# Hybrid decoder step on one core: where the bias rows are made, and which attention loads go out before the projection ends

## The chip, the core and the metric

The kernel runs on one core of a Trainium2 chip. The core has five engines with instruction streams of their own: TensorE (PE in the profile; its weight loads are PEld), VectorE (DVE), ScalarE (ACT), GpSimd (POOL) and SyncE (SP). SP computes nothing: it issues nearly all DMA transfers, in program order, so a transfer that has to wait holds those behind it. POOL issues the gathers from the paged cache. The metric is the time in microseconds of one execution on the device; shown is the median of several.

## The reference

One layer of a hybrid decoder trunk, for a prompt of 2048 tokens and for a sample group of 8 x 4 tokens with a paged cache of 8192 positions. Cut to what matters here:

```
h = rms_norm(x, pre_g);  z = h @ w_in            # 1024 -> 5632 columns, split into ca cb cg pu pg q k v sg mq mg
y_c = conv_branch(ca, cb)                        # GLU, causal depthwise conv (31), LayerNorm, swish, pointwise
y_p = pool_branch(pu)                            # causal means over 2/4/8/16, needs state_pool (8 x 15 rows) as history
y_s = stick_breaking(q, k, v, sb_bias)           # 8 heads x 64, strictly causal, z = q.k/8 + b_h
y_m = mem_attend(mq, mem_k, mem_v)               # 4 heads x 128, 256 memory tokens
mix = concat(y_c*silu(cg), y_p*silu(pg), y_s*silu(sg), y_m*silu(mg))
y   = rms_norm(x + rms_norm(mix @ w_out, post_g), final_g)

def sb_block(q, k, v, bias, q_pos, k_pos):       # stick-breaking attention
    z = einsum(q, k) * d**-0.5 + bias
    log_1m = where(k_pos < q_pos, log_sigmoid(-z), 0)
    a = exp(where(k_pos < q_pos, log_sigmoid(z) + reverse_cumsum(log_1m) - log_1m, -inf))
    return einsum(a, v)
```

Everything is float32; products are made from a high and a low part of each operand. Outputs are also the new keys and values and the conv and pool histories.

## The kernel before

The program has three stages. In the **projection**, PE multiplies 1024 prompt tokens at a time (part 0, then part 1) with one 128-column group of the combined weight after the other (`z_groups`, L819). At its start eight groups of the memory tokens are mixed in (`mem_tokens`, L418; their product is `mz`), and parameters and histories are loaded as rows and transposed by PE (`params_and_histories`, L474: tiles `ht` and products `hps`). A weight arrives by DMA as `wr`, ACT makes its high part `whi` and POOL its low part `wlo` (L241, L242); each kind has two buffers. Products leave PSUM through ACT and DVE and go to DRAM scratch: `qd` and `kd` (high and low parts of queries and keys), `vd` (values), `gsd` and `gcd` (gates), `ydw` (convolved rows), `mixd` (finished branch outputs). Beside the projection, the sample group's attention over the cache is interleaved step by step (gathers `kt` and `vt` by POOL, transposes `T` by DVE, scores `sSA` and values `sO` by PE).

The second stage is **prompt attention** (`sb_prompt`, L1312). It runs over 16 blocks: four head pairs `hp` times four query blocks `qb` of 512 rows. A block visits its key blocks `kc` from `qb` down to 0, and in each one four row pairs (two heads `hh`, and query tiles 0-1 or 2-3): scores `S` by PE into one of two PSUM banks, two sigmoids by ACT (`gam`, which has three buffers, and `be`; these are called the gates), scans `E` by DVE, a product by POOL, transposes `AT` by PE, a copy `at` by ACT, and the product `av` with the values. `sb_loader` (L1256) loads what a block needs: `load(hp, qb)` issues for each of two heads eight transfers (keys high `kh`, keys low `kl`, queries `Q`, and rows of `bd` that add the bias inside the product), and `values(hp)` one transfer of 1 MB (tile `V`). `bd` is a small DRAM tensor of bias rows, made once by `bias_rows` (L454): a load `brow`, a memset of `brows` on POOL, four small DVE copies and a store on SP. The third stage is the **output projection**.

Between the first two stages stands `sb_early` (L1298). When the sample's attention is done, its memory is closed and a pool `sbr` is opened in its place, while the projection is still running. `sb_early` loads block (0, 0) there and computes the first two row pairs' scores `Se` and gates `early` between the last matmuls of the projection. The pool `sb`, for all else, is opened when the projection's memory is closed, and its tiles take over addresses of projection tiles: who first writes such a tile waits until the old one's last reader is done.

The order on PE is the order of the code. On the other engines a scheduler orders the instructions. Work that is added as a task (`tasks.add`) is stepped in between the projection's steps. Each SP transfer reports on one of eight counters in turn, and waits until the eighth transfer before it has landed.

Of the kernel before, what the change touches and what calls it, by code (L numbers as in the profile page):

```python
# [9 lines left out]
F32R = mybir.dt.float32r  # L10
# [8 lines left out]
P = 128  # L19
# [43 lines left out]
KT = 2  # L63
# [29 lines left out]
def kernel(  # L93
# [9 lines left out]
    pe, act, dve, pool, sp = nc.tensor, nc.scalar, nc.vector, nc.gpsimd, nc.sync  # L103
# [155 lines left out]
    tasks = Tasks()  # L259
# [7 lines left out]
    def k4(name, shape, dt):  # L267
        return st.tile(shape, dt, tag="k4", name=name, bufs=K4)
# [7 lines left out]
    def later_stats():  # L276

        ahead = []
        for t in range(9):
            if t < 8:  # L280
                ahead.append(k4(f"xs1_{t}", [P, D], F32))
                sp.dma_start(ahead[-1], xp[PART + P * t : PART + P * (t + 1), :])
                yield
                yield
            if t:
                row_stats(ahead.pop(0), P, rs1[:, t - 1 : t])
                yield
        rstd(rs1)
# [165 lines left out]
    def bias_rows():  # L454

        b = zc.tile([NH, 1], F32, name="brow")
        sp.dma_start(b, sb_bias.rearrange("o h -> h o"))
        hl = zc.tile([NH, 2], F32R, name="bhl")
        t = k4("brows", [P, 2, 512], F32)
        pool.memset(t[: NH + 1], 1.0)  # L460
        for _ in range(3):
            yield
        dve.tensor_copy(hl[:, 0:1], b)
        dve.tensor_tensor(out=hl[:, 1:2], in0=b, in1=hl[:, 0:1].bitcast(F32), op=ALU.subtract)
        for x in range(2):
            dve.tensor_copy(t[:NH, x], hl[:, x : x + 1].bitcast(F32).to_broadcast([NH, 512]))
        sp.dma_start(bd, t[: NH + 1])
# [788 lines left out]
    def sb_loader(sbr):  # L1256

        KT, V = {}, {}

        def load(hp, qb):  # L1260
            tok = slice(512 * qb, 512 * qb + 512)
            Q = []
            for hh in range(2):
                pr = slice(64 * hh, 64 * hh + 64)
                kts = [(sbr if qb == 0 else KT["pool"]).tile([P, 512], F32R, tag=f"k{n}{qb}", name=f"k{n}{hp}_{qb}_{hh}",
                                                             bufs=2 if qb else 4) for n in "hl"]
                qt_ = sbr.tile([P, 2, 512], F32R, tag="Q", name=f"Q{hp}_{qb}_{hh}", bufs=4)
                for x in range(2):
                    hx = slice(64 * x, 64 * x + 64)
                    sp.dma_start(kts[0][hx].bitcast(F32), kd[hp, pr, 0, tok])  # L1270
                    sp.dma_start(qt_[hx, 0].bitcast(F32), qd[hp, pr, x, tok])
                sp.dma_start(kts[1][:64].bitcast(F32), kd[hp, pr, 1, tok])
                sp.dma_start(qt_[:64, 1].bitcast(F32), qd[hp, pr, 0, tok])
                sp.dma_start(kts[1][64:66].bitcast(F32), bd[2 * hp + hh])
                sp.dma_start(qt_[64:66, 1].bitcast(F32), bd[NH])
                KT[hp, hh, qb] = kts
                Q.append(qt_)
            if qb == 0 and hp:
                values(hp)
            return Q, KT, V  # L1280

        def values(hp):
            V[hp] = sbr.tile([P, 16, P], F32, tag="V", name=f"V{hp}", bufs=2)
            sp.dma_start(V[hp], vd[:, P * hp : P * (hp + 1)].rearrange("(t p) c -> p t c", p=P))

        return load, values

    def sb_scores(S, q2, w, Q, kts):
# [6 lines left out]
        act.activation(out=ga, in_=S[:, :, :w], func=AF.Sigmoid, scale=-1.0)  # L1295
        act.activation(out=be, in_=S[:, :, :w], func=AF.Sigmoid)  # L1296

    def sb_early(load, blk, sbr, bps, early):  # L1298

        room = sbr.tile([P, 16, P], F32, tag="V", name="early", bufs=2).rearrange("p (n j b) c -> p n j (b c)", n=4, j=2)  # L1300
        blk[0, 0] = load(0, 0)
        for _ in range(4):
            yield
        for hh in range(2):
            S = bps.tile([P, 512], F32, tag="AT", name=f"Se{hh}", bufs=2).rearrange("p (j k) -> p j k", j=2)
            Q, KT, _ = blk[0, 0]
            sb_scores(S, 0, 2 * P, Q[hh], KT[0, hh, 0])
            early[hh] = room[:, 2 * hh], room[:, 2 * hh + 1]
            sb_gates(S, 2 * P, *early[hh])
            yield  # L1310

    def sb_prompt(load, loaded, sb, bps, ops, zmp, early, values_of, flags, newest):  # L1312
# [14 lines left out]
        blocks = [(hp, qb) for hp in range(4) for qb in range(4)]  # L1327
# [88 lines left out]
                late.pop(0)[1]()  # L1416

        for bi, (hp, qb) in enumerate(blocks):
            if bi + 1 < len(blocks):
                loaded[blocks[bi + 1]] = load(*blocks[bi + 1])  # L1420
            if bi == 0:
                values_of(0)
            Q, KT, V = loaded[hp, qb]
            V = V[hp]
            gt = sb.tile([P, 512], F32, tag="sgt", name=f"sgt{hp}_{qb}", bufs=1)
            sp.dma_start(gt, gsd[hp, :, 512 * qb : 512 * qb + 512])
            carry = {}
            for kc in range(qb, -1, -1):
                base = step
                for q2 in (0, 2):  # L1430
                    for hh in range(2):
                        cost = 1.33 * (2 * q2 + 3) / 4 if kc == qb else 2.66
                        rest = score(hp, qb, kc, hh, q2, Q, KT, carry)
                        if len(pend) == 2:
                            pend.pop(0)()
                        pend.append(rest)
                        yield cost / 2
                        behind(step)
                        step += 1
                        yield cost / 2  # L1440
                for n, q2 in ((0, 0), (2, 2)):
                    late.append((base + n + TURN + SUM, lambda a=(hp, qb, kc, q2, V, gt): values(*a)))
                    for hh in range(2):
                        late.append((base + n + hh + TURN, lambda a=(hp, qb, kc, hh, q2): turn(*a)))
                late.sort(key=lambda x: x[0])
# [429 lines left out]
    with tc.tile_pool(name="mem", bufs=2, side="right") as mp:  # L1875
        M = {}
        xst = x_first(lambda n: mp.tile([P, D], F32, tag="xt", name=n, bufs=XB))
        for _ in range(X0):
            next(xst)
        tasks.add(xst)  # L1880
        params = params_and_histories(mp)
        for n, _ in enumerate(z_groups(0, GROUPS[0][:1])):
            tasks.step()
            if n in (0, 2):
                tasks.step()
            if n == 4:
                next(params)
            if X["done", 0] >= XM and not M:
                M["gen"] = mem_norm(mp, M)
                tasks.add(M["gen"])  # L1890
        for _ in M["gen"]:
            pass

        sp.dma_start(conv_sample[0][:, 0 : CH - TS, :], state_conv[0][:, TS:CH, :])
        sp.dma_start(pool_sample[0][:, 0 : PH - TS, :], state_pool[0][:, TS:PH, :])
        sp.dma_start(bias_bc, sb_bias[0].partition_broadcast(P))
        tasks.add(bias_rows())
        tasks.add(params)
        mem = mem_tokens(mp, M)
        for _ in z_groups(0, GROUPS[0][1:4], mem):  # L1900
            tasks.step()
        for _ in range(3):
            tasks.step()
# [11 lines left out]
    def main():  # L1915
        yield from z_groups(0, GROUPS[0][4:12])
        tasks.add(later_stats())
        yield from z_groups(0, GROUPS[0][12:])
        tasks.add(state_rows(0))
        yield from z_groups(1, GROUPS[1][:7])  # L1920
        tasks.add(sample_mem())
        yield from z_groups(1, GROUPS[1][7:-2])
        tasks.add(state_rows(1))
        yield from z_groups(1, GROUPS[1][-2:])
# [4 lines left out]
    due, blk, early = 0.0, {}, {}  # L1929
    sbr = bx = None  # L1930
    for cost in main():
        tasks.step()
        due += rate * cost
        while sample is not None and due >= 1.0:
            due -= 1.0
            try:
                next(sample)
            except StopIteration:
                sample = None
                sx.close()  # L1940
                bx = ExitStack()
                sbr = bx.enter_context(tc.tile_pool(name="sbr", bufs=1, side="right", reuse_waits="tile"))
                load, values_of = sb_loader(sbr)
                bps = bx.enter_context(tc.tile_pool(name="bps", bufs=1, space=PSUM, side="right", reuse_waits="tile"))
                starts = sb_early(load, blk, sbr, bps, early)
                next(starts)
                tasks.add(starts)
    tasks.drain()
# [185 lines left out]
    for n, x in enumerate(parts):  # L2134
# [15 lines left out]
        for k, p_ in enumerate(out_part(x) if n >= len(lead_) else lead if not n else ()):  # L2150
# [5 lines left out]
            if not n:  # L2156

                k, at_ = p_ % 4, p_ // 4
# [41 lines left out]
```

## Time and profile before

| | |
|---|---|
| median of 3 runs | 2349.55 us (2348.55, 2349.55, 2355.44) |
| the profiled execution | 2350.55 us |
| its span, first to last instruction | 2348.1 us |
| busy share of the span | PE 96%, DVE 70%, POOL 55%, ACT 48% |
| first matmul of prompt attention (`Se`) | 1475.9 us |
| granted PE clock, mean over the span | 0.990 |

Times in the views are microseconds from the start of the span. A row of instructions has start, duration, engine, line, operation, output <- inputs, and in brackets how long the engine was idle before it and what released it. A row of windows has the stretch and its length, then the busy time of PE, PEld, DVE, ACT and POOL (with instructions), the granted PE clock, the busy share of the DMA engines and GB/s. A row of waits has who waited for what, the total, the count and the longest.

### The profile page before, as it was taken

Reading aid. Unit: us, or ns where it says so; the run is one execution under the profiler, and the core shown is the slowest. Engines: PE = TensorE matmul, PEld = TensorE weight load, DVE = VectorE, ACT = ScalarE, POOL = GpSimd, SP = SyncE. Lnnn points to the kernel's source line nnn. Section 1 sums busy time; section 2 is a strip of 40 time slices with the busy share of each in tenths; the row PEclk is TensorE's granted clock in tenths of the full one; section 3 lists DMA queues with packets and bytes.
Section 4 is the critical chain, followed back from the end, with each engine's and each line's share of the span. In section 5 each row is a group of like instructions: output and inputs, shape, how many; then the busy total and the mean of one; then the engine's idle time right before and its main releaser. Section 6 shows DMA issues by size and latency. Waiting matters only on the chain. (4 is left out here: it accounts for less than half of the span.)

```text
span 2348.1 us, 43432 instructions
## 1 busy us (share of the span) xinstructions
PE 2246.9 (96%) x16512; PEld 1812.3 (77%) x16512; DVE 1654.7 (70%) x2247; ACT 1125.3 (48%) x2031; POOL 1296.6 (55%) x1410
## 2 busy tenths in 40 slices
PE   7899999999999999999999999799999899999997
PEld 7898888888888777777777777566666667788775
DVE  5332686969757764478787867787877766686997
ACT  6232343242442322224242234699999985453553
POOL 3454545556474656545555454488988863432333
PEclk9999999999999999999999999899999999999999
DMA  6589977878778999987877884576544206976774
GB/s 216 172 269 308 348 264 260 284 261 274 265 249 308 310 355 337 333 278 274 310 255 243 300 274 139 144 208 192 153 126 137 79 19 224 291 229 191 240 246 150
DMA packets 338188, 558.31 MB, mean 238 GB/s; under 512 B 29163, under 2 KB 213611, under 8 KB 321581
## 3 DMA queue, kind: packets, MB, share of 16 engines
q1 hardware_dynamic: 282604, 286.83, 39.5%
q0 software_dynamic: 55376, 268.72, 32.3%
q8 instruction: 130, 2.13, 0.4%
q14 instruction: 78, 0.63, 0.1%
HBM read 465.35 MB, written 90.72 MB: 237 GB/s over the span
## 5 line engine op out<-in xcount | busy, mean ns | idle before, releaser
L990 DVE STREAM_TRANSPOSE T<-kt 128x1024 f32<-128x1024 f32 x256 | 308.7, 1226 | 185.1 <-PE sSA L1003 175.4
L957 POOL DMA_INDIRECT vt<-in_cache_v_dram,idv x256 | 252.4, 986 | 255.4 <-PE sO L1042 194.4
L642 DVE SCALAR_TENSOR_TENSOR cacc<-U,par,cacc 128x512 f32<-128x512 f32 x480 | 360.0, 750 | 11.0
L1372 POOL TENSOR_TENSOR be<-be,E 128x512 f32<-128x512 f32 (+4 forms) x316 | 301.3, 964 | 28.0 <-DVE E L1363 13.8
L1363 DVE TENSOR_TENSOR_SCAN E<-gam,cr,ZM 128x513 f32<-128x513 f32 x192 | 232.7, 1265 | 29.6 <-ACT gam L1295 26.4
L957 POOL DMA_INDIRECT kt<-in_cache_k_dram,idk x128 | 128.2, 1001 | 201.5 <-DVE T L990 159.0
L2019 PE MATMUL acc<-wohi,mh 128*128 128x512 f32 (+1 forms) x480 | 193.5, 403 | 1.1 <-ACT mh L1743 1.1
L2019 PE MATMUL acc<-wolo,mh 128*128 128x512 f32 (+1 forms) x480 | 189.6, 395 | 0.0
L2019 PE MATMUL acc<-wohi,ml 128*128 128x512 f32 x448 | 178.8, 399 | 7.2 <-DVE ml L1754 7.2
L1391 PE MATMUL AT<-ident,be 128*128 128x128 f32 x1082 | 150.0, 278 | 24.3 <-ACT at L1393 17.9
L1295 ACT ACTIVATE gam<-S 128x1024 f32<-128x1024 f32 (+1 forms) x158 | 162.4, 1028 | 17.7 <-PE S L1292 14.3
L1393 ACT COPY at<-AT 128x512 f32<-128x512 f32 (+1 forms) x288 | 161.3, 647 | 18.7 <-PE AT L1391 18.6
L1391 PEld LDWEIGHTS AT<-ident,be 128*128 128x128 f32 x1082 | 118.7, 141 | 66.6 <-issue 28.8
L1296 ACT ACTIVATE be<-S 128x1024 f32<-128x1024 f32 (+1 forms) x158 | 161.6, 1023 | 0.0
L1291 PE MATMUL S<-kh,Q 128*128 128x512 f32 (+1 forms) x316 | 132.0, 422 | 13.2 <-DMA kh<-kd 13.2
L1003 PE MATMUL sSA<-T,W 128*32 128x128 f32 x4096 | 138.4, 276 | 2.0 <-DVE T L990 1.6
L1360 DVE TENSOR_TENSOR_SCAN E<-gam,ZM 128x384 f32<-128x384 f32 (+1 forms) x124 | 95.5, 814 | 60.3 <-ACT gam L1295 57.4
L1403 PE MATMUL av<-at,V 128*64 128x256 f32 (+1 forms) x1152 | 136.3, 377 | 0.0
L1003 PEld LDWEIGHTS sSA<-T,W 128*32 128x32 f32 x4096 | 104.8, 109 | 36.8 <-issue 29.4
L1754 DVE TENSOR_TENSOR ml<-mr,mh 128x512 fp32r<-128x512 f32 x108 | 92.4, 863 | 44.1 <-ACT mh L1743 43.3
L1042 PE MATMUL sO<-vt,saT 128*32 128x512 f32 x1024 | 122.1, 592 | 0.0
L1403 PEld LDWEIGHTS av<-at,V 128*64 128x64 f32 x1152 | 76.1, 137 | 56.7 <-issue 24.8
(590 smaller groups left out, 6176.6 us busy)
## 6 DMA issues: line engine op xcount, KB each, us to landing
mr<-mixd SPq DMA_DIRECT2D x32, 512.0 KB
Q<-qd SPq DMA_DIRECT2D x96, 128.0 KB
mr<-mixd SPq DMA_DIRECT2D x48, 256.0 KB
xtp<-in_x_prompt_dram SPq DMA_DIRECT2D x16, 512.0 KB
kh<-kd SPq DMA_DIRECT2D x64, 128.0 KB
ws<-in_w_out_dram SPq DMA_DIRECT2D x16, 512.0 KB
wsd<-ws SPq DMA_DIRECT2D x16, 512.0 KB
msd<-mr SPq DMA_DIRECT2D x32, 256.0 KB
```

The source lines that it names most:

```text
L642: dve.scalar_tensor_tensor(out=ps, in0=U[:, a + k : a + k + H], scalar=wd[:, k : k + 1], in1=ps, op0=ALU.mult, op1=ALU.add)
L957: pool.indirect_dma_start(out=dst, out_offset=None, in_=rows, in_offset=bass.IndirectOffsetOnAxis(ap=idx, axis=0))
L990: S["turn"] = dve.transpose(T[:, 2 * hh : 2 * hh + 2].rearrange("p s j t -> p (s j t)"), kt[:, 2 * hh : 2 * hh + 2].rearrange("p s j d -> ...
L1003: pe.matmul(sSs[n][32 * g : 32 * g + 32, P * ml : P * (ml + 1)], lhsT=W[:, jj, :], rhs=T[:, :, jj, :], start=i == 0, stop=i == 3, tile_pos ...
L1295: act.activation(out=ga, in_=S[:, :, :w], func=AF.Sigmoid, scale=-1.0)
L1296: act.activation(out=be, in_=S[:, :, :w], func=AF.Sigmoid)
L1363: dve.tensor_tensor_scan(out=E[:, j][:, ::-1], data0=g_[:, j][:, ::-1], data1=ZM[:, 0:1].to_broadcast([P, 513]), initial=carry[hh, q2][:, ...
L1372: newest.append(pool.tensor_tensor(out=be[:, j, :m], in0=be[:, j, :m], in1=E[:, j, 513 - w : 513 - w + m], op=ALU.mult).ins)
L1391: pe.transpose(ap_[:, n : n + P], A[hp, qb, kc, hh, qt][:, P * r : P * (r + 1)], ident)
L1393: act.copy(at[:, :n], ap_[:, :n])
L1403: pe.matmul(av[64 * hh : 64 * hh + 64, c], lhsT=V[:, 4 * kc + r, 64 * hh : 64 * hh + 64], rhs=ats.pop((hp, qb, kc, hh, q2, r)), start=dg a ...
L2019: pe.matmul(o[:rows], lhsT=m[a][:, k, :rows], rhs=W[prod, 4 * h + k][w], start=not cont and h == k == n == 0, stop=h == 1 and k == 3 and n ...
```

## The change

Three edits. The task `bias_rows` is added later: not at the end of the first group but behind the first value groups. In `sb_early`, blocks (0, 0) and (0, 1) are both loaded, and the values of the first head pair behind them; `sb_prompt` no longer loads these itself. For that the key buffers are shared out anew: query block 0 used to have four buffers of each kind in `sbr` and blocks 1 to 3 two each in `sb`; now `sbr` holds two for block 0 (even head pairs) and two for block 1, and `sb` two for block 0 of odd head pairs (slot 4) and two each for blocks 2 and 3. The amount of memory is the same.

```diff
@@ load(hp, qb) in sb_loader
-                kts = [(sbr if qb == 0 else KT["pool"]).tile([P, 512], F32R, tag=f"k{n}{qb}", name=f"k{n}{hp}_{qb}_{hh}",
-                                                             bufs=2 if qb else 4) for n in "hl"]
+                slot = qb if qb or hp % 2 == 0 else 4
+                kts = [(sbr if slot < 2 else KT["pool"]).tile([P, 512], F32R, tag=f"k{n}{slot}", name=f"k{n}{hp}_{qb}_{hh}",
+                                                              bufs=2) for n in "hl"]
@@ sb_early
-    def sb_early(load, blk, sbr, bps, early):
+    def sb_early(load, values, blk, sbr, bps, early):
         room = sbr.tile([P, 16, P], F32, tag="V", name="early", bufs=2).rearrange("p (n j b) c -> p n j (b c)", n=4, j=2)
-        blk[0, 0] = load(0, 0)
+        for n in range(2):
+            blk[0, n] = load(0, n)
+        values(0)
@@ sb_prompt
-            if bi + 1 < len(blocks):
+            if bi + 1 < len(blocks) and blocks[bi + 1] not in loaded:
                 loaded[blocks[bi + 1]] = load(*blocks[bi + 1])
-            if bi == 0:
-                values_of(0)
@@ behind the first group
         sp.dma_start(bias_bc, sb_bias[0].partition_broadcast(P))
-        tasks.add(bias_rows())
         tasks.add(params)
@@ main()
         yield from z_groups(0, GROUPS[0][4:12])
         tasks.add(later_stats())
+        tasks.add(bias_rows())
         yield from z_groups(0, GROUPS[0][12:])
@@ the call
-                starts = sb_early(load, blk, sbr, bps, early)
+                starts = sb_early(load, values_of, blk, sbr, bps, early)
```

How this moves instructions, at three places. First, SP's queue in the first microseconds of the projection, where the pooling history `ht15_0` is loaded. Before:

```order
L492 DMA ht30_4_658<-in_state_conv_dram 120x512
L233 DMA wr0q3_689<-in_w_in_dram 128x8x128
L435 DMA mkd_67<-mhlk0_693 128x512
L467 DMA bd_69<-brows_638 9x1024
L492 DMA ht15_0_721<-in_state_pool_dram 120x512
L450 DMA out_10_dram<-mnat0_726 128x2x128
```

And now:

```order
L492 DMA ht30_4_653<-in_state_conv_dram 120x512
L233 DMA wr0q3_684<-in_w_in_dram 128x8x128
L435 DMA mkd_67<-mhlk0_688 128x512
L492 DMA ht15_0_711<-in_state_pool_dram 120x512
L450 DMA out_10_dram<-mnat0_716 128x2x128
```

The store of the bias rows to `bd` no longer stands ahead of the history's load. Second, SP's queue behind the first value groups, where the store stands now (`xs` are rows of the prompt's second half for `later_stats`, `wr0cg` and `wr0pg` weights); before, the same rows stood there without `bd`:

```order
L282 DMA xs1_1_2724<-in_x_prompt_dram 128x1024
L233 DMA wr0cg0_2506<-in_w_in_dram 128x8x128
L467 DMA bd_69<-brows_2694 9x1024
L282 DMA xs1_2_2809<-in_x_prompt_dram 128x1024
L282 DMA xs1_3_2904<-in_x_prompt_dram 128x1024
L233 DMA wr0pg0_2674<-in_w_in_dram 128x8x128
```

Third, SP's queue at the end of the projection, behind the loads of block (0, 0). In `kh0_1_0` the numbers are head pair, block and head. Before:

```order
L744 DMA gsd_61<-sg1sg3_0_14738 128x512
L744 DMA gcd_60<-sg1cg3_1_14778 128x512
L564 DMA mixd_63<-mo1_3_512_14791 128x4x128
L1271 DMA Q0_1_0_14885<-qd_57 64x512
L649 DMA ydw_62<-acc1_3_1_14854 128x512
```

```order
L744 DMA gsd_61<-sg1sg3_1_14828 128x512
L1284 DMA V0_14905<-vd_59 128x16x128
L1270 DMA kh0_1_0_14883<-kd_58 64x512 x2
L1272 DMA kl0_1_0_14884<-kd_58 64x512
L1274 DMA kl0_1_0_14884<-bd_69 2x512
```

And now (the sixteen loads of block (0, 1) stand ahead of it, the last four of them shown):

```order
L1273 DMA kl0_1_1_14738<-kd_58 64x512
L1274 DMA Q0_1_1_14739<-qd_57 64x512
L1275 DMA kl0_1_1_14738<-bd_69 2x512
L1276 DMA Q0_1_1_14739<-bd_69 2x512
L1285 DMA V0_14748<-vd_59 128x16x128
L744 DMA gsd_61<-sg1sg3_0_14762 128x512
L744 DMA gcd_60<-sg1cg3_1_14802 128x512
L564 DMA mixd_63<-mo1_3_512_14815 128x4x128
L744 DMA gsd_61<-sg1sg3_1_14852 128x512
L649 DMA ydw_62<-acc1_3_1_14878 128x512
L1272 DMA Q0_2_0_14939<-qd_57 64x512 x2
L1274 DMA Q0_2_0_14939<-qd_57 64x512
```

The keys of block (0, 1) and the values moved ahead of five stores of the projection's last results, and the loads of block (0, 2) come right behind these.

## The prediction

> **What bounds the kernel now.** I read the page's busy shares first, then what TensorE (PE) waited for, then windows of the stages that the change touches, and last the rows in order of time around the two longest waits there.
>
> ```profile
> PE 2246.9 (96%) x16512; PEld 1812.3 (77%) x16512; DVE 1654.7 (70%) x2247; ACT 1125.3 (48%) x2031; POOL 1296.6 (55%) x1410
> PE S L1291 <- DMA kh<-kd: 13.2, 1, 13.2
> PE hps L510 <- DMA ht<-in_state_pool_dram: 6.4, 1, 6.4
> 180.00:300.00 120.00, 120.00 (x1112) 107.42 (x1115) 61.61 (x76) 36.79 (x79) 59.31 (x53) 1.00 0.94 326
> 1500.00:1550.00 50.00, 45.46 (x325) 33.16 (x325) 41.41 (x52) 44.16 (x66) 36.06 (x53) 0.96 0.55 136
> ```
>
> PE is busy for 96% of the span, so the time is PE's work plus PE's waits. In the projection it never pauses (120.00 of 120 us) although the DMA engines are 0.94 busy, so what is won before it is still won behind it. In prompt attention PE (45.46 of 50) and ACT (44.16) limit each other. Each wait row gives a total, a count and the longest: two single waits of PE on a DMA, 13.2 and 6.4 us. The change moves what stands ahead of both.
>
> **Part 1: the bias rows leave the early queue.** Rows are start, duration, engine (SPq is SP's queue of DMA issues).
>
> ```profile
> 64.50 0.58 SPq L435 DMA_DIRECT2D mkd<-mhlk  x1
> 71.59 0.28 SPq L467 DMA_DIRECT2D bd<-brows  x1
> 71.97 0.34 SPq L492 DMA_DIRECT2D ht<-in_state_pool_dram  x1
> 70.82 0.74 DVE L466 COPY brows<-bhl 8x512 f32<-8x512 f32 x2
> 67.10 0.38 PE L251 MATMUL z0q<-xhi,whi0q 128*128 128x288 f32 x1
> 68.65 0.29 PE L251 MATMUL z0q<-xhi,wlo0q 128*128 128x288 f32 x1
> 75.35 1.03 PE L510 MATMUL hps<-ident,ht 120*128 120x120 f32 x4 [6.40 <-DMA ht<-in_state_pool_dram]
> 76.46 0.59 PE L251 MATMUL z0q<-xhi,whi0q 128*128 128x288 f32 x1
> 79.48 0.41 PE L251 MATMUL mz<-mhi,whi0mem 128*128 128x256 f32 x1
> 66.00:68.00 2.00, 2.00 (x19) 2.00 (x19) 0.00 (x0) 1.11 (x2) 0.00 (x0) 1.00 0.95 275
> 68.00:70.00 2.00, 0.94 (x8) 0.71 (x6) 1.32 (x1) 0.61 (x2) 1.99 (x1) 1.00 0.22 80
> 76.00:78.00 2.00, 2.00 (x10) 2.00 (x10) 1.18 (x5) 0.00 (x0) 0.00 (x0) 0.50 0.95 264
> ```
>
> SP issues in order. After mkd (ends 65.08) it stands for 6.5 us at the store of bd, which waits for DVE's copies (70.82 to 71.56); the load of ht, the pooling history, comes behind it, and PE's transposes need it. Without bd, ht can go at 65.1. From its issue to PE's start it took 75.35 − 71.97 = 3.4 us, then on idle DMA engines. At 65.1 the weights and mkd are in front of it: the engines are 0.95 busy to 68 and done near 68.4 (0.22 of the next 2 us). 240 KB at 275 GB/s are 0.9 us, so I take 69.4, against 68.8, when PE has finished its group of twelve. The wait falls from 6.4 to about 0.6. Bounds: 68.5 (no wait left) and 71.5 (the busy engines, then the full 3.4 us).
>
> The slow clock goes with the wait. Behind 6.4 us of idling the granted clock is 0.50 (window 76 to 78): the twelve matmuls from 76.46 to 79.48 take 3.02 us, the twelve from 67.10 some 1.68. With the six transposes (75.35 to 76.46, about half of it too much) that is 1.9 us. Hence mz starts at 69.4 + 4.13 − 1.9 = 71.6 in place of 79.48, 7.9 us earlier, and runs on the full clock: its 24 matmuls, 3.44 us here, take 2.81 later (87.34 to 90.15), 0.6 us more. What is late next is the next weight:
>
> ```profile
> 79.48 1.04 ACT L241 CAST whi0q<-wr0q 128x1024 fp32r<-128x1024 f32 x1 [10.84 <-PE z0q L251]
> 80.60 2.39 POOL L242 TENSOR_TENSOR wlo0q<-wr0q,whi0q 128x1024 fp32r<-128x1024 f32 x1 [10.23 <-ACT whi0q L241]
> 82.92 0.34 PE L251 MATMUL z0q<-xhi,whi0q 128*128 128x384 f32 x1
> 83.27 0.34 PE L251 MATMUL z0q<-xhi,wlo0q 128*128 128x384 f32 x1
> 87.34 0.28 PE L251 MATMUL mz<-mhi,whi0mem 128*128 128x256 f32 x1
> 90.15 0.34 PE L251 MATMUL z0q<-xhi,whi0q 128*128 128x384 f32 x1
> ```
>
> ACT's cast starts when PE leaves the old weight and wlo0q is there 3.5 us later (79.48 to 82.99); PE wants it for the third matmul behind mz, 2.81 + 0.35 us on (82.92 to 83.27), so it waits 0.3 us. Part 1 is **−8.2 us**; with ht at 71.5 and a PE that cools again, −4; with no wait at all, −8.8.
>
> The work itself is not saved but moved to the value groups near 240 us: one memset on POOL (0.94 us in its old place), two small DVE copies (0.74), one store of 36 KB. I cost it at nothing. PE runs without a pause there, DVE idles 4.9 us behind the transposes after which the copies now stand, and SP is held there anyway:
>
> ```profile
> 237.05 8.45 SPq L282 DMA_DIRECT2D xs<-in_x_prompt_dram  x2
> 244.13 1.25 DVE L990 STREAM_TRANSPOSE T<-kt 128x1024 f32<-128x1024 f32 x1 [4.88 <-PE sSA L1003]
> 239.52 0.95 POOL L957 DMA_INDIRECT kt<-in_cache_k_dram,idk  x1 [3.34 <-DVE T L990]
> 254.97 2.37 DVE L990 STREAM_TRANSPOSE T<-kt 128x1024 f32<-128x1024 f32 x2 [7.52 <-PE sSA L1003]
> ```
>
> Behind bd on SP are two loads of xs and then the weight wr0pg. POOL too waits there (3.34 us ahead of the gather in front of which the memset now stands). If the cover were gone, the copies' 0.7 us and the memset's 0.9 would be the price.
>
> **Part 2: keys and queries of the second block, and the first values, go out earlier.**
>
> ```profile
> 1463.14 0.52 SPq L1270 DMA_DIRECT2D kh<-kd  x1
> 1472.00 0.25 SPq L1275 DMA_DIRECT2D Q<-bd  x1
> 1484.70 0.39 SPq L1284 DMA_DIRECT2D V<-vd  x1
> 1485.18 4.15 SPq L1270 DMA_DIRECT2D kh<-kd  x2
> 1493.78 0.24 SPq L1274 DMA_DIRECT2D kl<-bd  x1
> 1481.34 0.40 PE L1292 MATMUL S<-kl,Q 66*128 66x512 f32 x1
> 1494.92 0.55 PE L1291 MATMUL S<-kh,Q 128*128 128x256 f32 x1 [13.18 <-DMA kh<-kd]
> 1484.26 1.02 ACT L1296 ACTIVATE be<-S 128x1024 f32<-128x1024 f32 x1
> 1500.21 1.03 ACT L1295 ACTIVATE gam<-S 128x1024 f32<-128x1024 f32 x1 [0.89 <-ACT at L1393]
> 1487.15 1.00 DVE L1360 TENSOR_TENSOR_SCAN E<-early,ZM 128x128 f32<-128x128 f32 x2 [1.80 <-DMA gsd<-sg1sg]
> 1488.07 3.99 DVE L1360 TENSOR_TENSOR_SCAN E<-gam,ZM 128x384 f32<-128x384 f32 x4
> 1514.20 0.37 PE L1291 MATMUL S<-kh,Q 128*128 128x256 f32 x1
> 1484.00:1494.00 10.00, 0.00 (x0) 0.00 (x0) 5.91 (x8) 3.11 (x4) 6.03 (x10) 0.50 0.89 222
> ```
>
> The sixteen loads of the first block are issued from 1463.14 to 1472.25, 9.1 us. The second block's sixteen now follow at once, to about 1481.4, then V. Its first half is issued by 1477 and its second by 1481.4, and 3.4 us more are 1484.8. PE is done with the first block at 1481.7, but not free: its score bank is released only by ACT's be, which ends at 1485.28. So keys are no longer what it waits for. Behind that the third pair of gate buffers must be released by DVE's scans. The scans wait 1.80 us for a store of a projection tile; in the changed order no scan carries such a wait, so they end at 1490.3 instead of 1492.06. The gates of block (0, 1)'s third row pair, at 1500.21 now, could then start at 1490.4: **at best −9.8 us**, from where ACT runs back to back as it does now.
>
> But V now stands ahead of five stores that were issued around it before: gsd, gcd, mixd, gsd, ydw, 256 KB each. In the changed order ACT's first two copies "at" lie on tiles that mixd and ydw read, and wait for these stores. V's landing: the last kl waits for the eighth transfer before it, which is V, until 1493.78, 9 us behind V's issue; the kh issued right behind V freed PE at 1494.92, 1.1 us later still. So V issued near 1481.6 lands near 1490.6, and the stores after it. By bytes: 1 MB, five stores and some 0.3 MB still on the way are 2.6 MB, at 222 GB/s of this stretch 11.7 us from 1481.6, at the 275 of the early stretch 9.5; ydw lands between 1491 and 1495, I take 1493. Then the second "at" copy ends near 1493.5 and the gates that started at 1500.21 start at 1493.6: **−6.6 us**. Bounds: −9.8 (stores not held by V) and −2.5 (ydw at 1497, which is 2.6 MB at 170 GB/s).
>
> The Trainium skill, "DMA: Bandwidth & Descriptors", section "Queues, rings and completion order", speaks against this part: each DMA engine takes a queue's descriptors in ring order, and a completion is reported only after all earlier writes of that engine. By it the stores can't report before V is in, and the sum holds −6.6; without it −9.8. The kh behind V, reported 1.1 us after V, agrees.
>
> Next late could be block (0, 2): its third load waits for V's completion (eight in flight), then 14 issues of 0.58 us and 3.4 us give 1502.5; PE needs it at 1514.20 − 6.6 = 1507.6. Hidden, with 5 us to spare. The order of matmuls on PE is the same in both kernels, and the buffers are only shared out differently: nothing else moves on the path.
>
> **Sum.** Against the profiled execution (2350.55 us: span 2348.1 and 2.45 around it): 2350.55 − 8.2 − 6.6 = 2335.75. That execution is 1.0 above the median 2349.55, so the median should be **2335 us**, 0.6% faster.
>
> **Rivals.** (a) *The stores are not held*: parts at their best, −8.8 − 9.8: 2331. For it: 1 MB is only 3.8 us at 275 GB/s, and V may be in by 1487 where it has less beside it. Against: its 9 us before, and the 1.1 us. (b) *The stall moves from keys to stores*: ydw lands only at 1500, when the gates start today, and part 2 gives nothing: 2341. For it: SP itself stood 3.5 us behind V (kh x2, 4.15). (c) *The early gain is not kept*: the projection's DMA engines (0.94 busy) and not PE set its pace, PE's full windows being slack that fits itself to the gathers, so only part 2 is left: 2349.55 − 6.6 = 2343. Against: PE 120.00 of 120 without a wait. (d) *Slower*: the moved store holds SP and the memset holds POOL near 240 us. The memset needs a buffer whose old stores are on the way (the xs issues took 8.45 us there), and the cache gather stands behind it on POOL. The gather issued at 239.52 feeds the transpose at 254.97, 15.5 us on; 1 MB at this stretch's 326 GB/s is 3.2 us, with as much queued twice ahead of it 9.6. So 6 to 12 us are slack, and a hold beyond 6 us costs PE what it exceeds them by. It decides from 6 + 14.8 = 21 us; at 27 us the time is 2335 + 21 = 2356. The longest issue seen there is 8 us, worth 2 by this. (e) *No effect at all* would need both waits to come back in full; the early queue excludes it for ht.
>
> **How the numbers follow.** Chances: forecast (2332 to 2338.5) 0.50, (a) 0.14, (b) 0.18, (c) 0.10, (d) 0.04, something between (c) and no change 0.04. What counts as no change is 0.3%, 7 us. Faster: forecast, (a), (b) and a little over a third of (c): 0.86. Within: the rest of (c) and of the last: 0.10. Slower: 0.04. The range, 2329.5 to 2343, holds (a), the forecast and (b) and the ends of the bounds (−18.6 gives 2331, −4 − 2.5 gives 2343), with 1.5 us below for what a run differs by (the lowest of the three is 1.0 under the median); the forecast's own is 2332 to 2338.5.
>
> **What would show it.** Right: ht issued near 65, PE's wait for it under 1.5 us and no clock of 0.50 at 76 to 78; all of PE earlier by about 8 us at 300 us and still so at 1460; behind the first block PE waiting 3 us for ACT or its bank, not for kh; ACT's "at" released by mixd or ydw some 9 to 11 us behind V's issue; the shift at the end of attention about 15 us. Wrong: a new wait of PE near 240 us, the shift shrinking along the projection, or block (0, 2)'s keys waited for.

## The result, and the profile after

| comparison with the kernel before, on one chip each | changed kernel, us | before, us | ratio (95% interval) |
|---|---|---|---|
| first, 4 and 4 executions | 2330.34 | 2349.05 | 0.9916 (0.9896 to 0.9935) |
| second, 6 and 19 | 2334.39 | 2350.22 | 0.9931 (0.9917 to 0.9945) |
| third, 5 and 17 | 2333.75 | 2351.72 | 0.9928 (0.9915 to 0.9940) |

The change makes the kernel 0.7 to 0.8% faster. All 15 executions of the changed kernel have a median of 2333.75 us, 70 of the kernel before one of 2350.7: 17.0 us less. The forecast was 2335 us, 14.55 less. The first four executions alone had said 18.7, and lie lower than the later eleven: two of them, at 2327.9, are 4.7 us under the lowest of those. The profiled execution of the changed kernel took 2334.90 us (span 2333.2), 15.65 under the profiled one of before.

The page's busy shares and PE's longest waits on the stages that the change touches:

```profile
PE 2248.1 (96%) x16512; PEld 1810.3 (78%) x16512; DVE 1659.4 (71%) x2247; ACT 1125.2 (48%) x2031; POOL 1293.5 (55%) x1410
PE S L1292 <- ACT be L1297: 3.2, 2, 2.9
PE hps L510 <- DVE us_s L512: 2.5, 1, 2.5
```

The 13.2 us for keys and the 6.4 us for the history are gone. In their places stand 2.9 us for ACT's gates and 2.5 us in front of the same transposes. The early rows in order of time, of the changed kernel:

```profile
64.90 0.39 SPq L492 DMA_DIRECT2D ht<-in_state_pool_dram  x1
70.33 0.84 DVE L512 COPY us_s<-hps 128x120 f32<-128x120 f32 x4
71.18 0.60 PE L510 MATMUL hps<-ident,ht 120*128 120x120 f32 x4 [2.49 <-DVE us_s L512]
73.43 0.28 PE L251 MATMUL mz<-mhi,whi0mem 128*128 128x256 f32 x1
77.09 0.44 PE L251 MATMUL z0q<-xhi,wlo0q 128*128 128x384 f32 x1 [0.34 <-POOL wlo0q L242]
76.00:78.00 2.00, 1.66 (x11) 1.34 (x10) 1.97 (x3) 1.61 (x3) 1.77 (x3) 1.00 0.00 0
```

The load of `ht` goes out at 64.90 (71.97 before, 65.1 forecast), `mz` starts at 73.43 (79.48 before, 71.6 forecast), the clock from 76 to 78 us is 1.00 (0.50 before), and the new wait for `wlo0q` is 0.34 us, where 0.3 was forecast. The rows at the start of attention:

```profile
1470.36 0.28 PE L1292 MATMUL Se<-kh,Q 128*128 128x256 f32 x1
1476.11 0.38 SPq L1285 DMA_DIRECT2D V<-vd  x1
1476.58 1.94 SPq L744 DMA_DIRECT2D gsd<-sg1sg  x1
1479.09 0.42 SPq L564 DMA_DIRECT2D mixd<-mo  x1
1480.81 0.82 SPq L649 DMA_DIRECT2D ydw<-acc  x1
1479.07 0.38 PE L1292 MATMUL S<-kh,Q 128*128 128x256 f32 x1 [2.91 <-ACT be L1297]
1484.30 0.48 ACT L1396 COPY at<-AT 128x384 f32<-128x384 f32 x1 [2.47 <-DMA mixd<-mo]
1485.64 0.50 ACT L1396 COPY at<-AT 128x384 f32<-128x384 f32 x1
1485.65 0.19 POOL L1371 COPY cr<-E 128x2 f32<-128x2 f32 x1 [0.20 <-DMA ydw<-acc]
1486.00 1.07 ACT L1296 ACTIVATE gam<-S 128x1024 f32<-128x1024 f32 x1
1500.59 0.37 PE L1292 MATMUL S<-kh,Q 128*128 128x256 f32 x1
```

PE waits for ACT, not for keys. ACT's first copy waits 2.47 us for `mixd`. Its second, at 1485.64, has nothing in brackets: it follows two of ACT's gates without a pause. `ydw` lands just in time for it, since a small copy on POOL waits for `ydw` to 1485.65. The gates of the third row pair start at 1486.00 (1500.21 before), the scores of block (0, 2) at 1500.59 (1514.20 before).

The shift of PE's same instructions between these two profiles is 6.05 us at `mz`, 5.58 at `Se`, 13.61 at block (0, 2) and 14.9 at the end of the span. By this pair part 1 would be worth 5.6 us, where 8.2 was forecast, and part 2 8.0, where 6.6 was. The experiments show that the first of these comes of comparing two single executions.

### The profile page after: what moved, and what is told of

It reads as the page before. It is cut to its first block, busy times and chain, and to the rows that moved or that the text cites. A ratio compares the mean times of both kernels' runs of the same rounds, so it can differ in the third digit from the quotient of the medians.

```text
span 2333.2 us, 43434 instructions
## 1 busy us (share of the span) xinstructions
PE 2248.1 (96%) x16512; PEld 1810.3 (78%) x16512; DVE 1659.4 (71%) x2247; ACT 1125.2 (48%) x2031; POOL 1293.5 (55%) x1410
```

## The experiments

One table for all of them. `mz`, `Se` and `S(0,2)` are the starts of the matmuls that begin at 79.48, 1475.94 and 1514.20 us in the first profile of before; the last column is the time from `Se` to `S(0,2)`, the stretch in which part 2 acts. One profile each. A ratio is to the kernel before on the same chip; the medians of before on the chips were 2349.05 to 2351.72 us, so medians of rows from different chips compare to 1 or 2 us only.

| kernel | median, us (executions) | ratio (95% interval) | mz | Se | S(0,2) − Se |
|---|---|---|---|---|---|
| before | | | 79.48 | 1475.94 | 38.26 |
| before_again | 2352.74 (11) | 1.0004 (0.9993 to 1.0015) | 79.14 | 1479.05 | 37.41 |
| bias_only: part 1 alone | 2340.63 (12) | 0.9966 (0.9953 to 0.9979) | 71.42 | 1470.12 | 37.97 |
| loads_only: part 2 alone | 2342.82 (8) | 0.9964 (0.9952 to 0.9976) | 79.82 | 1482.17 | 30.70 |
| changed kernel | 2330.34 (4) | 0.9916 (0.9896 to 0.9935) | 73.43 | 1470.36 | 30.23 |
| again: changed kernel | 2334.39 (6) | 0.9931 (0.9917 to 0.9945) | 72.27 | 1470.59 | 30.98 |
| again2: changed kernel | 2333.75 (5) | 0.9928 (0.9915 to 0.9940) | 71.09 | 1469.52 | 29.63 |
| values_late | 2332.39 (6) | 0.9930 (0.9910 to 0.9950) | 71.42 | 1470.48 | 29.97 |
| values_first | 2332.84 (6) | 0.9924 (0.9897 to 0.9951) | 72.03 | 1470.31 | 28.87 |
| values_first2 | 2334.36 (5) | 0.9922 (0.9909 to 0.9935) | 72.30 | 1475.11 | 28.88 |
| values_actq | 2331.84 (6) | 0.9923 (0.9895 to 0.9950) | 70.72 | 1466.17 | 28.73 |
| values_actq2 | 2334.80 (6) | 0.9926 (0.9911 to 0.9941) | 72.63 | 1472.43 | 29.02 |
| hist_early | 2337.93 (12) | 0.9956 (0.9938 to 0.9973) | 70.17 | 1471.56 | 32.48 |
| both | 2335.04 (8) | 0.9934 (0.9912 to 0.9955) | 70.17 | 1476.47 | 28.86 |

**How far do executions of one program differ?** The changed kernel and the kernel before, unaltered.

> The changed kernel once more, unaltered, to see how far its executions differ among themselves. Theory: the profiled execution (span 2333.2 us) holds two stretches of halved clock in its last 320 us (6.8 and 3.4 us long, worth some 5 us) that the executions with spans of 2325.5 and 2326.2 us do not have; this profile, if its span is near 2326, shows no such stretch behind 1500 us, or one at most, and its instructions up to 2000 us stand where they stood, within 1 us. The median is 2328 to 2331 us. Rival: the executions differ already in attention or in the projection (by several us at 1470 or at 1560 us), then the spread has nothing to do with the clock of the last part.

> The kernel before once more, unaltered, for a second profile of it. Of the other kernels' shifts against its first profile, those in the projection differ by far more than the edits can explain: two kernels that share everything up to 1460 us with another one stood 5 to 6 us apart there. Theory: inside the projection an execution loses or wins 0.5 to 3 us at single places where ScalarE waits for the store of nat0k or VectorE for the store of mixd (DMA landings, 0.94 of the engines busy), so this second profile stands 2 to 6 us off the first at 1470 us, with the jumps at such places; the early wait for the pooling history is 6 to 6.5 us as before, and the wait for keys behind the first block 11 to 15 us. Time 2350. Rival: the projection repeats to 1 us, and the differences came from the edits.

Two rows of the second profile of before, and one of part 2 alone, which is the program of before up to its early loads:

```profile
1479.05 0.28 PE L1291 MATMUL Se<-kh,Q 128*128 128x256 f32 x1
PE S L1291 <- DMA kh<-kd: 12.8, 1, 12.8
```

```profile
1482.17 0.28 PE L1292 MATMUL Se<-kh,Q 128*128 128x256 f32 x1
```

Up to its early loads this is one program, and it reaches `Se` at 1475.94, 1479.05 and 1482.17 us: 6.2 us apart, and the first profile of before, on which every term was worked out, is the earliest of the three. The theory of `again` did not hold: its profile stands up to 3.3 us off the first one between 200 and 300 us, comes back to 0.2 us at `Se`, and its span, 2333.5 us, is not one of the short ones. So the spread does not sit in the clock of the last part alone, and what made two of the first four executions short was not seen. Where an execution falls behind in the projection is seen at a few places. Rows of `again`, of values_first2 and of `both`:

```profile
307.25 0.44 PE L251 MATMUL z0mg<-xhi,whi0mg 128*128 128x384 f32 x1 [1.64 <-DVE sg0pg L734]
306.21 0.62 DVE L623 SCALAR_TENSOR_TENSOR po<-py,par,sg0pg 128x384 f32<-128x384 f32 x1 [5.65 <-DMA mixd<-po]
```

```profile
310.21 0.44 PE L251 MATMUL z0mg<-xhi,whi0mg 128*128 128x384 f32 x1 [1.90 <-DVE sg0pg L734]
309.17 0.62 DVE L623 SCALAR_TENSOR_TENSOR po<-py,par,sg0pg 128x384 f32<-128x384 f32 x1 [6.57 <-DMA mixd<-po]
```

```profile
149.69 0.41 ACT L716 ACTIVATE zt0k<-z0k 128x288 f32<-128x288 f32 x1 [2.99 <-DMA out_dram<-nat0k]
```

DVE and ACT wait for a buffer whose store has not landed, and PE for them, by 0 to 2.4 us at each place, in one execution and not in the next. With three profiles of one program 6.2 us apart, one trace prices a term early in the program to some 3 us once it is carried to 1470 us; the mean over several does better.

**Part 1 alone.** The one task moved:

```diff
-        tasks.add(bias_rows())
         tasks.add(params)
@@ main()
         tasks.add(later_stats())
+        tasks.add(bias_rows())
```

> The kernel before with the first part of the change alone: the bias rows are made in mid-projection, all loads of prompt attention go out as before. Theory from the two traces: the second group of transposes of the pooling history waits for VectorE's copies out of the first group's bank (to about 71.2 us) and not for the load, so the matmuls that started at 79.48 us start at 73.4, 6.0 us earlier; 5.6 us of it are left at 1470 us; the wait of 13.2 us for keys behind the first block stands as before. Time: 2349 less 5.6 to 6, 2343 us. Rival, the forecast's own term: 8.2 us, 2341. Rival, the gain is not kept through the projection: 2349, with the shift at 1470 us near zero.

```profile
64.07 0.39 SPq L492 DMA_DIRECT2D ht<-in_state_pool_dram  x1
69.18 0.60 PE L510 MATMUL hps<-ident,ht 120*128 120x120 f32 x4 [1.31 <-DMA ht<-in_state_pool_dram]
69.50 0.84 DVE L512 COPY us_s<-hps 128x120 f32<-128x120 f32 x4
59.62 1.00 POOL L719 TENSOR_TENSOR hl0q<-zt0q,hl0q 128x384 fp32r<-128x384 f32 x1 [4.62 <-ACT whi0mem L241]
60.58 2.37 POOL L242 TENSOR_TENSOR wlo0mem<-wr0mem,whi0mem 128x1024 fp32r<-128x1024 f32 x1
```

This refutes the theory that came out of the first pair of traces. Here the transposes run at 69.18, before DVE's copies `us_s` have even started (69.50), so these copies did not hold them: in the changed kernel's first profile the releaser named was only the event that came last. What is left is the load, which seven of the nine profiles with this order name. The transposes start 5.1 us behind its issue here and 6.3 there. The wait for keys behind the first block stands, with 12.93 us. The time, 2340.63 us, is nearer to the forecast's 2341 than to the 2343 of the theory.

**Part 2 alone.** The bias rows back in their old place, the early loads kept.

> The second part of the change alone: keys and queries of block (0, 1) and the first values are loaded early, the bias rows are made where they were. Theory from the two traces: PE waits 6.4 us for the pooling history near 69 us as before; the gates of the third row pair of block (0, 1), at 1500.2 us before, start 8.6 us earlier, near 1491.6; block (0, 2)'s scores 8.0 us earlier; the time is 2349 less 8 to 10, 2339 to 2341 us. Rival, the forecast's own term: 6.6 us, 2342.5. Rival, the parts are not independent (without the early gain the loads meet other traffic): the shift at 1560 us differs by more than 1.5 us from 8.0.

The time, 7.4 us under before, is the forecast's own figure (by the ratio it is 8.5). From `Se` to block (0, 2) it takes 30.70 us, like the changed kernel; PE waits 6.07 us for the history, as before. The two parts do not hang on each other: in ratios they take off 0.34% and 0.36%, together 0.70%, and both at once 0.69 to 0.84%.

**Where the values stand.** First behind the five stores, as before the change:

```diff
         for n in range(2):
             blk[0, n] = load(0, n)
-        values(0)
@@ sb_prompt
                 loaded[blocks[bi + 1]] = load(*blocks[bi + 1])
+            if bi == 0:
+                values_of(0)
```

> The changed kernel with the first values loaded where they were before, behind the five stores of projection tiles; keys and queries of block (0, 1) stay early. Theory (the stores stand in the rings behind the 1 MB of values and so land late): without the values ahead of them mixd and ydw land by 1483 us, ScalarE's copies at, which waited 2.47 us for mixd and then to 1485.6 for ydw, wait for the scans or for nothing, and the gates of the third row pair start near 1484.3 in place of 1486.0 us: 1.7 us less. That holds if the values, issued near 1480, land by 1487, when PE first needs them. Rival: the stores are late by themselves, since the keys' transfers fill the engines; then the copies wait as long and nothing changes. Rival: the values now are late; PE waits for V by 1 to 3 us near 1488 and the time is 1 to 2 us longer than the changed kernel's.

```profile
1477.35 0.40 SPq L564 DMA_DIRECT2D mixd<-mo  x1
1478.48 0.83 SPq L649 DMA_DIRECT2D ydw<-acc  x1
1479.53 0.48 SPq L1285 DMA_DIRECT2D V<-vd  x1
1482.47 0.52 ACT L1395 COPY at<-AT 128x384 f32<-128x384 f32 x1
1489.17 0.87 PE L1405 MATMUL av<-at,V 128*64 128x256 f32 x8 [2.16 <-DMA V<-vd]
```

The theory came true in part, and so did one rival. The copies no longer wait: 1482.47 with nothing in brackets, 1.8 us earlier than in the changed kernel. But the gates of the third row pair start at 1485.35 (1486.00 there, 1484.3 in the theory), now behind PE's scores, and the values land only at 1489.2, 9.6 us behind their issue, so that PE waits 2.16 us for them. What is left over is small, 29.97 us to block (0, 2) against 29.6 to 31.0.

Then the values ahead of the second block's keys, and on ScalarE's queue, each twice:

```diff
-        for n in range(2):
-            blk[0, n] = load(0, n)
-        values(0)
+        blk[0, 0] = load(0, 0)
+        values(0)
+        blk[0, 1] = load(0, 1)
```

```diff
-            sp.dma_start(V[hp], vd...)
+            (nc.scalar if hp == 0 else sp).dma_start(V[hp], vd...)
```

> The changed kernel with the first values issued between the loads of the first and the second block, near 1467.5 us, 9 us earlier. Theory: they land near 1476, the stores behind them are not held, so ScalarE's copies do not wait; but SP stands some 3 us at the third or fourth load behind them, as it did before the change (4.15 us), so the second block's last loads are issued near 1480 and land near 1483; PE, which now waits for ScalarE until 1479, waits for keys or queries of the second block to 1482 or so. The two about cancel: the gates of the third row pair within 1.5 us of the changed kernel's, time 2333 to 2336. Rival: SP is not held, the copies' wait is saved in full: 2332. Rival: keys late by 5 us or more: 2338.

> The changed kernel with the first values (1 MB) loaded as early as now, but issued on ScalarE's queue; SP's five stores then do not stand behind them on one queue. Theory: mixd and ydw were late because they stood behind the values on SP's queue; on two queues they land before ScalarE's copies need them, the copies do not wait (2.5 us in the changed kernel), and the gates of the third row pair start 0.7 to 1.7 us earlier, as with the values loaded late; the values, early as they are, are not waited for. Time 2332 to 2333. Rival: it is the 1 MB of traffic, not the place in the queue; then the copies wait 1.5 us or more and nothing changes (2334).

> The changed kernel a third time, beside two versions with the first values elsewhere, on one chip. Theory: 2334 us (2332 to 2336); ScalarE's copies wait 2.4 to 5.3 us for mixd or ydw, attention's shift (from 1470 to 1600 us against the kernel before) is 6 to 9.6 us. Rival: the lower times of its first measurement (median 2330) come back.

> The first values ahead of the second block's keys, again, beside the changed kernel. Theory: PE waits 3.6 us for a query tile of the second block in place of 2.9 for ScalarE, the copies wait under 0.5 us, attention's shift is 10 to 11 us (11.0 in its first profile) and the median 1.5 to 4 us below the changed kernel's. Rival: within 1.5 us of it.

> The first values on ScalarE's queue, again, beside the changed kernel. Theory: attention's shift against the kernel before is 10 to 11.5 us (11.2 in its first profile), 2 to 4 more than the changed kernel's, since the stores no longer stand behind the values; the median is 1.5 to 4 us below the changed kernel's. Rival: its first profile was a lucky one in the projection (10 us ahead there); then the medians are within 1.5 us.

Rows of values_first, then the values' issue in values_actq:

```profile
1466.77 0.38 SPq L1285 DMA_DIRECT2D V<-vd  x1
1479.93 0.41 SPq L564 DMA_DIRECT2D mixd<-mo  x1
1482.92 0.48 ACT L1396 COPY at<-AT 128x384 f32<-128x384 f32 x1 [0.47 <-DMA mixd<-mo]
1479.71 0.58 PE L1292 MATMUL S<-kh,Q 128*128 128x256 f32 x1 [3.60 <-DMA Q<-qd]
```

```profile
1453.22 0.39 ACTq L1285 DMA_DIRECT2D V<-vd  x1
```

Where the values are in long before, `mixd` lands 3.0 us behind its issue (1479.93 to 1482.92). Where they stand right ahead it takes 5.2 (1479.09 to 1484.30), and the first store behind them occupies SP for 1.94 us. PE's wait for the second block is 3.60 in place of 2.91 us, so the keys were hardly late: in values_first2 the same 3.60 us end with ACT's gates. All four profiles need 28.7 to 29.0 us from `Se` to block (0, 2). The three of the changed kernel and the one of part 2 alone, with the values between keys and stores, need 29.6 to 31.0, on the mean 1.5 more. So the values do hold something up there. In the time it can't be told apart: 2334.36 and 2334.80 us against 2333.75 for the changed kernel on the same chip, so in both second runs the rival came true and the theory, 1.5 to 4 us less, did not. On ScalarE's queue the load went out 13 us before `Se`, where the changed kernel issues it 5.8 us behind, so that run does not tell the place in the queue from the traffic.

**The history's load earlier.** Its tile gets a buffer of its own and is issued behind the second convolution history; `both` adds the late values.

```diff
-                hts.append(mp.tile([P, 512], F32, tag="ht", ..., bufs=3))
+                hts.append(mp.tile([P, 512], F32, tag="ht", ..., bufs=3) if len(hts) < 2 else k4("htp", [P, 2, 512], F32)[:, 0])
...
             if n == 2:
-                load()
+                load(), load()
```

> The changed kernel with the pooling history's load issued three places earlier on SP, right behind the second convolution history (near 62.2 us, ahead of a weight and of mkd), into a buffer of its own. In the traces so far PE's transposes of it start 5.1 to 6.3 us behind its issue (69.18 to 71.18 us) and wait 1.2 to 2.5 us. Theory: that wait is for the load alone; issued two us earlier it is in by 68 us, PE does not wait, and the matmuls behind it start 1.2 to 2.5 us earlier than in the changed kernel. But of an early shift of 6.8 to 9.7 us at 200 us all four kernels without the early hold had 5.4 to 5.8 left at 1470 us, so no more than 0.5 us of it should be left there, and the time stays that of the changed kernel, 2333 to 2335 us. Rival 1: PE waits for VectorE's copies us_s, as the changed kernel's first profile has it; then the wait stays at 2.5 us. Rival 2: what is won before the projection is kept; the shift at 1470 us is 1.2 to 2.5 us larger and the time 2332.

> The pooling history's load three places earlier (as above) and the first values loaded where they were before the change, everything else as in the changed kernel. Theory: the second is worth 1.4 to 2 us in attention, the first nothing that lasts: 2332 to 2333 us. Rival, the early gain is kept: 2330 to 2331.

```profile
67.96 0.57 PE L510 MATMUL hps<-ident,htp 120*128 120x120 f32 x4
70.22 1.02 POOL L719 TENSOR_TENSOR hl0q<-zt0q,hl0q 128x384 fp32r<-128x384 f32 x1 [0.63 <-PE z0q L251]
71.27 0.53 SPq L721 DMA_DIRECT2D qd<-hl0q  x1
71.89 0.56 SPq L233 DMA_DIRECT2D wr0mem<-in_w_mem_kv_dram  x1
76.82 1.04 ACT L241 CAST whi0mem<-wr0mem 128x1024 fp32r<-128x1024 f32 x1 [5.22 <-DMA wr0mem<-in_w_mem_kv_dram]
78.19 0.44 PE L445 MATMUL mt<-ident,mzt 128*128 128x128 f32 x2 [2.35 <-ACT mzt L439]
1488.30 0.48 ACT L1396 COPY at<-AT 128x384 f32<-128x384 f32 x1 [5.27 <-DMA ydw<-acc]
```

PE does not wait for the history any more (67.96, nothing in brackets), but the gain is spent 10 us later. The edit also changed the order on POOL: a weight's low part now runs ahead of `hl0q`, so SP stands at the store of `qd` until 71.27 (66.00 in the changed kernel) and issues the next weight behind it at 71.89 (70.15). ACT waits 5.22 us for that weight and PE 2.35 for ACT. The edit changed attention too: ACT's first copy now waits 5.27 us for `ydw`, where the changed kernel's waits 2.47 for `mixd`; why its buffer hangs on that store now is not shown. At 2337.93 us the kernel is some 4 us above the median of the changed kernel, which was measured on other chips. The ranges of the ratio overlap only a little (0.9938 to 0.9973 against 0.9917 to 0.9945 of `again`), and neither theory nor rival had such a loss; `Se` 1 us later than the mean and 2.1 us more in attention account for part of it. `both`, at 2335.04, is no gain either: its projection ends 6 us later than the mean, by waits such as those for the weight and for `nat0k` (the row of `both` above), against a stretch of 28.86 us in attention.

## Why the prediction was right, and where it was wrong

**What failed.** The forecast's gain was 14.55 us; it is 17.0 by all executions, and was 18.7 in the first four, whose median of 2330.34 us lies below the forecast's own 2332 to 2338.5; the two later medians lie inside. The mechanism of both parts held. The term that was mis-sized is part 2's 6.6 us, and the step behind it is that ACT's second copy waits for `ydw` until 1493. What holds ACT is its first copy, waiting for `mixd`; `ydw` is in by 1491.2 in the times of before and holds ACT no further, so the part is worth 7.5 us. Of the 2.4 us that the whole gain was put too low, this is 0.9; about 1 us stays open, and so does what made two of the first four executions short.

**Part 1, 8.2 us: right on the mean, and a single pair of profiles would have refuted it.** In the nine profiles that have part 1 and the history's load where it puts it, `mz` starts at 71.92 us on the mean, where 71.6 was forecast and the three others stand at 79.48. `Se` comes at 1470.6 on the mean of the nine and at 1479.05 on that of the three: 8.5 us. With the nine from 1466.2 to 1475.1 and the three 6.2 us apart this is good to some 2 us. The time of part 1 alone says 9.6 (8.0 by the ratio). Rival (c), that the projection takes the gain back, is not borne out: by ACT's casts of the weights, the mean of the nine stands 7.6 us ahead of the mean of the three at 79 us, 8.5 at 181, 8.7 at 975 and 8.5 at 1418. Against the first profile of before alone the same casts would show the gain shrinking, from 7.5 to 5.4 us, which the prediction named as a sign of being wrong.

Three steps behind it failed all the same.

- *The wait of 0.6 us for the load.* The transposes start at 68.5 to 71.2, at 69.6 on the mean, with 69.4 forecast. That this agrees is partly luck, since two errors cancel: the load goes out at 64.2 on the mean, not 65.1, and the transposes start 5.4 us behind it, not 4.3. PE too is there earlier and waits 1.0 to 2.5 us. I had missed a new order on DVE. Rows of before, then of part 1 alone:

```profile
59.51 0.31 DVE L502 COPY par<-pps 128x144 f32<-128x144 f32 x1 [1.21 <-PE pps L501]
60.22 0.35 DVE L718 CAST hl0q<-zt0q 128x384 fp32r<-128x384 f32 x1
61.68 2.35 POOL L242 TENSOR_TENSOR wlo0mem<-wr0mem,whi0mem 128x1024 fp32r<-128x1024 f32 x1
64.08 0.39 PE L251 MATMUL mz<-mhi,wlo0mem 128*128 128x256 f32 x1 [1.48 <-POOL wlo0mem L242]
```

```profile
58.77 0.35 DVE L718 CAST hl0q<-zt0q 128x384 fp32r<-128x384 f32 x1
60.06 0.31 DVE L502 COPY par<-pps 128x144 f32<-128x144 f32 x1 [0.94 <-PE pps L501]
```

  The cast `hl0q` now stands ahead of copies that wait for PE, POOL makes `wlo0mem` 1.1 us earlier (60.58 above), and PE's wait of 1.48 us for it goes. PE and the issue of `mkd` (63.41 us against 64.50) come 1.1 us earlier, and with `mkd` the load behind it, so PE waits for the load all the same.
- *"PE never pauses in the projection."* The window that I quoted (120.00 of 120 us) does not hold in every execution: the second profile of before has 118.65 there. In the changed kernel the same window reads

```profile
180.00:300.00 120.00, 118.73 (x1075) 104.59 (x1068) 68.05 (x85) 36.27 (x78) 59.98 (x55) 1.00 0.93 325
```

  and the waits at 150 and 307 us differ from one execution to the next.
- *Terms good to 0.1 us.* The sum was worked out against one profiled execution whose projection was the fastest of three.

The moved task itself costs nothing that the traces show near 230 us, where it runs (its store goes out at 233.62 in the changed kernel; its load and two of its four small copies stay early, at 71 to 78 us), as forecast; rival (d) did not come.

**Part 2, 6.6 us: right in its mechanism, a little small.** From `Se` to block (0, 2) the kernel without it takes 37.4 to 38.3 us (three profiles, mean 37.9), with it 29.6 to 31.0 (four, mean 30.4; `hist_early`, whose first copy waits for another store, is left out): 7.5 us. At the gates of the third row pair, the place of the forecast, it is more: they start 23.4 to 24.3 us behind `Se` without the part (mean 23.9) and 15.5 to 15.7 with it, 8.3 us earlier. Where 0.8 us of this goes before block (0, 2) was not followed. PE's wait for ACT is there (2.91, forecast 3).

The step that failed is the hold by the stores. I let the second copy wait for `ydw` until 1493 in the times of before, from 1491 to 1495, and the gates start at 1493.6. In the changed kernel the first copy is the one that waits, 2.47 us for `mixd`; the second follows in ACT's own order. `ydw` came by 1485.65, which is 1491.2 there, 9.5 us behind the values' issue: the lower bound, by 275 GB/s. The gates start at 1486.00, which is 1491.6 there.

My reason for the stores' lateness is shown in part. The rule of the Trainium skill that I cited, "DMA: Bandwidth & Descriptors", section "Queues, rings and completion order", fits 3.0 us from issue to landing without the values and 5.2 behind them; but some 1.6 us more is SP itself, which stands 1.94 us at the store behind the values where the same store takes 0.35 with the values well ahead (`values_first`), and no run separates order in the rings from mere traffic. Rival (a), stores not held, is what the kernels with the values early enough reach: 9.0 us (37.9 to 28.9), with 9.8 forecast as the bound. Rival (b) did not come. Block (0, 2)'s keys were not waited for.

**The sum.** 8.5 and 7.5 are 16.0 us by the means of the profiles, 14.8 by the forecast's terms, 17.0 by the medians. The rest, 1.0 us, is not assigned: from block (0, 2) to the end the changed kernel takes 831.9 to 832.6 us in three profiles, and the kernel before 831.3 and 833.9. Against the pooled median the predicted 2335 is 1.3 us high; the gain itself was put 2.4 us low, and the first median of before, 1.2 us under that of 70 executions, hides half of that.

## What to carry to other kernels

Before a term of a few microseconds is carried through a thousand, look at a second profile of the same program: here one instruction near 1476 us moved by 6 us between executions, nearly as much as a whole term. A load or a store that is moved on an issue queue moves everything behind it, and what counts is the next item that someone waits for: taking the bias store out was worth 8 us, and moving one load three places forward cost some of it again, because a weight slipped back. Look also at what a large load stands ahead of: here 1 MB of values in front of small stores made them land 2 us later, which cost 1.5 us in attention; well ahead of them it did not, and behind them PE waited for the values instead. In the kernel's time these orders could not be told apart.

## What the runs showed of the hardware that was not expected

**The clock fell behind a wait that was shorter than others that left it alone.** In the changed kernel PE waits 2.49 us at 71 us and keeps its full clock (the row 76 to 78 above, and 1.00 in 60 to 80); in `again` 2.12 us, with the same. In values_first2 it waits 1.97 us at the same place:

```profile
69.23 0.60 PE L510 MATMUL hps<-ident,ht 120*128 120x120 f32 x4 [1.97 <-DMA ht<-in_state_pool_dram]
70.00:76.00 6.00, 6.00 (x39) 6.00 (x38) 3.31 (x7) 1.41 (x3) 2.40 (x1) 0.72 0.57 163
```

and the clock over the next 6 us is 0.72. So the length of a wait does not decide it alone. The Trainium skill, "TensorE: Matmul & The Clock Gate", section "What's actually happening", has the activity window run freely, so that one kernel's slow stretches differ from run to run; these two rows agree with that.

**A releaser can be named wrongly.** A wait is put down to the event that came last. In the changed kernel's first profile that was a copy on DVE which ended just as PE's wait did; only a second execution, in which the copy began after the waiting instruction, showed that it had nothing to do with it. In `values_first` the name is that of yet another DVE instruction, `mhlk`, for the same wait.
